# A hybrid decoder layer whose tile context schedules on the timeline machine model

## The chip, the cores and the metric

The kernel runs on one core of one Trainium2 chip. The metric is the device time of one execution in microseconds (us); lower is better. The time of the kernel before is the median of three runs.

## The reference

One layer of a decoder trunk: 1024 tokens, width 1024, float32. Both head groups read the same normalised input through one projection; after them come an output projection, a gated feed-forward network of width 2816 and a gated embedding, each added to the residual, and a last norm.

```python
hn = rms_norm(x, norm_mix_w[i])
proj = (hn @ w_in[i]).astype(jnp.float32)
...
y_ret = retention(q, k, v)            # 4 heads of 128, chunks of 128 tokens
y_ret = head_norm(y_ret) * ret_norm_w[i] * silu(ret_gate)
y_rw = rwkv7_mix(proj[..., RET_COLS:], ...)   # 8 heads of 64, a state per head over all tokens
mixed = jnp.concatenate([y_ret, y_rw], axis=-1)
x = x + mixed @ w_o[i]
hf = rms_norm(x, norm_ffn_w[i])
x = x + (silu(hf @ w_gate[i]) * (hf @ w_up[i])) @ w_down[i]
hp = rms_norm(x, norm_ple_w[i])
x = x + (p[i] @ w_ple_up[i]) * sigmoid(hp @ w_ple_gate[i])
return rms_norm(x, final_norm_w)
```

## The kernel before

Channels lie on the partitions, tokens along the free dimension, and the tokens are taken in two halves of 512. A float32 value of the dense products is split into a high and a low part (`split`, lines 246 to 248: ScalarE copies the high part at L247, VectorE or GpSimd subtracts it at L248), and a product is three matmuls: high times high, high times low, low times high. All matmuls are issued at L189 (`mm`), transposes at L193 (`tr`), all transfers on SyncE's queue.

There are two kinds of work in the first part of the program. The dense products (`dense`, tile names d<-x, d<-rr, d<-mix, d<-hT in the trace) need only weights and an operand in SBUF. The eight RWKV groups (`rwkv_group`: a pair of heads, half of the tokens) and the eight retention tasks (`retention`: a head, half of the tokens) are chains of small steps: a matmul, an operation of VectorE or ScalarE on its result, the next matmul. In a group these are, by the names of the PSUM tiles, ss, pb (two), then a row-by-row inverse on VectorE alone (L643 and L645, 31 steps of two operations), pk (two), bo, pq (five), psm (two), pw (two), pmq (two) and pkh (two), then eight steps of the state (pZ from the state Sn, copies of the state at L748 and L749 into STb, the transpose pS, the scaled copy Sn at L753), and at the end py and pyt. Retention goes through rtp (two), rsc, rU, rY and ryt. Each group and each retention task ends with a store into mixd (L783, L874), from which `mix_load` fetches the operands of the output projection (d<-mix).

The order of the program is written by `weave` (line 127). It counts matmul time in `pe` and, by constants such as `WAIT`, `INVW` and `MIDW`, decides after which dense matmuls the next step of a group or of a task is emitted. It runs while the program is traced and knows nothing of the scheduler. What comes out is one list of instructions over all engines.

From this list the tile context makes the queues of the engines when it closes. Its scheduler plays the program on a model of the machine: whenever an engine of the model can take an instruction, it gets, of those whose operands the model has finished and for which there is a buffer, the first in the order of the program (moved up by the few `tc.high_priority` blocks, mainly for the weight loads, and held by `tc.issue_after` in two places). So an instruction whose operand is not finished on the model is passed by later ones, and the order reached on the model is the order of the queue on the chip. Which buffer of a pool a tile gets is settled in the same way. Before the change the model is the default one.

After the RWKV part come the second halves of the feed-forward network with its down products (`down`, tile pd), and the embedding's gate (pg) with the last norm (`finish`).

Of the kernel before, what the change touches and what calls it, by code (L numbers as in the profile page):

```python
# [13 lines left out]
PSUM = bass.MemoryType.PSUM  # L14
DRAM = bass.MemoryType.DRAM
# [14 lines left out]
# columns of the packed constants  # L30
# [7 lines left out]
# columns of the packed parameter vectors  # L38
# [43 lines left out]
# a group may enter a stage once the group before it has reached another  # L82
# [44 lines left out]
def weave(groups, tasks, dg, count, pe, done):  # L127
    """Emit the groups' instructions as their operands become ready, then those of the first ready task, dense work in between.

    groups: (name, generator, dense items it needs), in order; tasks: name -> (generator, dense items, names that come before it)"""  # L130
    n = len(groups)
    ready, stage = [0.0] * n, [0] * n
    now, seen, mixed = 0.0, pe[0], 0.0
    tasks = dict(tasks)
    due = {k: 0.0 for k in tasks}
    last = STAGE["done"]
    while True:
        step = None
        for i, (name, g, need) in enumerate(groups):
            if stage[i] == last:  # L140
                continue
            if i and stage[i - 1] < STAGE[AFTER[STAGES[stage[i]]]]:
                break
            if count[0] >= need and ready[i] <= now and f"low{name[-1]}" in done:
                step = i
                break
        task = None
        for k, (g, need, before) in tasks.items():
            if max(due[k], mixed if k[:3] == "mix" else 0.0) <= now and count[0] >= need and all(x in done for x in before):
                task = k  # L150
                break
        if step is not None:
            st, wait = next(groups[step][1])
            stage[step] = STAGE[st]
            if stage[step] == last:
                done.add(groups[step][0])
            now += pe[0] - seen
            ready[step] = now + wait * (WAIT1 if groups[step][0][-1] == "1" else WAIT)
        elif task is not None:
            wait = next(tasks[task][0], None)  # L160
            now += pe[0] - seen
            if wait is None:
                mixed = now + MIXW if task[:3] == "mix" else mixed
                done.add(task)
                del tasks[task]
            else:
                due[task] = now + wait * (RWAIT1 if task[:3] == "ret" and task[-1] == "1" else RWAIT)
        elif min(stage) == last and not tasks:
            return
        else:  # L170
            if next(dg, True):
                now += 100.0
            now += pe[0] - seen
        seen = pe[0]
# [3 lines left out]
def tile_hybrid_layer(ctx: ExitStack, tc: tile.TileContext, I, out):  # L178
# [66 lines left out]
    # a float32 value as two float32r parts that add up to it exactly  # L245
# [9 lines left out]
    def dense(items, count, done, eng):  # L255
        """items: (weights [128, 512 n] in float32, variants); a variant (gate, columns, operands, use) gives use() the sum over
        its 128 columns of weights^T operand, once the names in gate are done. Yields after a few matmuls, whether it had to wait."""
# [41 lines left out]
    def rsqrt(y, x, tmp):  # L299
        """y = x ** -0.5 in place of x for positive x: a guess from the exponent, then Newton's steps"""  # L300
        V.tensor_scalar(out=tmp.bitcast(I32), in0=x.bitcast(I32), scalar1=1, scalar2=None, op0=ALU.logical_shift_right)
        V.tensor_scalar(out=y.bitcast(I32), in0=tmp.bitcast(I32), scalar1=-1.0, scalar2=1597463007.0, op0=ALU.mult, op1=ALU.add)
        V.tensor_scalar(out=x, in0=x, scalar1=-0.5, scalar2=None, op0=ALU.mult)
        for _ in range(3):
            V.tensor_tensor(out=tmp, in0=y, in1=y, op=ALU.mult)
            V.tensor_tensor(out=tmp, in0=tmp, in1=x, op=ALU.mult)
            V.scalar_tensor_tensor(out=y, in0=tmp, scalar=1.5, in1=y, op0=ALU.add, op1=ALU.mult)

    # RMS norm over the channels, which lie on the partitions
# [8 lines left out]
    def norm_rs(acc, parts, R):  # L318
        """R = 1 / sqrt(mean + eps) in all partitions; parts: room for the sums"""
        split(acc, *parts)  # L320
        norm_mm(*parts, R)
# [12 lines left out]
    def raw_split(raw, w, hi, lo):  # L334
        """the parts of raw times the norm's weight"""
        act(hi, raw, AF.Copy, scale=w)  # L336
        return V.scalar_tensor_tensor(out=lo, in0=raw, scalar=w, in1=hi.bitcast(F32), op0=ALU.mult, op1=ALU.subtract)

    def slabs(name):
        """[128, (kt, hi | lo, 512 tokens)]"""  # L340
        return slab.tile([P, KT, 2, HS], F32R, tag="s", name=name)
# [7 lines left out]
    # =================== input norm, input projection, RWKV and retention ===================  # L349
    with ExitStack() as s1:  # L350
# [22 lines left out]
        # x times the norm's weights; 1 / rms comes in when the projections leave PSUM  # L373
# [57 lines left out]
        def lerp(h, ps, i, t):  # L431
            """token shift with mu of tile i, token half h"""
            g = evac("pn")
            V.tensor_tensor(out=g, in0=ps, in1=Rx[h], op=ALU.mult)
            ps = g
            act(t, ps, AF.Copy, scale=pv(OMU + i))
            mu = pv(MU + i)
            if h == 0:
                edge[i] = sm.tile([P, 1], F32, tag="edge", name="edge", bufs=6)
                act(edge[i], ps[:, HS - 1:HS], AF.Copy, scale=mu)  # L440
            else:
                V.tensor_tensor(out=t[:, 0:1], in0=t[:, 0:1], in1=edge.pop(i), op=ALU.add)
            V.scalar_tensor_tensor(out=t[:, 1:HS], in0=ps[:, 0:HS - 1], scalar=mu, in1=t[:, 1:HS], op0=ALU.mult, op1=ALU.add)
# [24 lines left out]
        def low(h):  # L468
            """decay, in-context rate and gate of all heads from their low-rank parts"""
# [14 lines left out]
            # the high part beside the low one: one pass over 128 rows for both  # L484
# [34 lines left out]
        # block-diagonal holders; the zero blocks are written once  # L519
# [33 lines left out]
        def rwkv_group(p, hf):  # L553
            """a pair of heads over 8 chunks of 64 tokens; yields (stage, ns until the next matmuls can start)"""
# [11 lines left out]
            def headsum(ps, t):  # L566
                """sum of t over the channels of a head"""
# [11 lines left out]
            # decay and normaliser  # L579
# [35 lines left out]
            # products inside the chunks  # L615
# [25 lines left out]
            # inverse of the unit triangular blocks of 32 rows  # L641
# [32 lines left out]
            # two chunks at a time, then each head's rows to their place  # L674
# [20 lines left out]
            # merge to 64 rows  # L695
# [16 lines left out]
            # the chunk as an affine map: S' = P_C (M S + Kf V), y = Q S + Hy V  # L712
# [9 lines left out]
            for g in range(2):  # L722
# [8 lines left out]
                # M and Q take the room of their factor  # L731
# [6 lines left out]
            # the state (before P_C, transposed) and the output: [(h, v), (k | t)] of each chunk  # L738
# [18 lines left out]
            # head norm in token-major form, bonus, gate  # L757
# [34 lines left out]
        def retention(h, a):  # L792
            """a head over four chunks of 128 tokens; yields ns until the next matmuls can start"""
# [26 lines left out]
            # the scores take the room of v, the states that of k, the output that of the token-major k  # L820
# [13 lines left out]
            # the state before each chunk  # L834
# [25 lines left out]
            # (qs y - mean) / sqrt(var + eps) with the moments of y  # L860
# [16 lines left out]
        # =================== the dense products in an order that feeds the groups ===================  # L877
# [3 lines left out]
        # the embedding's operands, in the room of the retention  # L881
# [20 lines left out]
        def project(ct, use, halves):  # L902
            n = len(items)

            def var(h):
                def fin(ps):
                    # the first sums wait in PSUM for 1 / rms
# [31 lines left out]
        # the last heads' first token half before their second one: the operands of the output projection take its room  # L939
# [13 lines left out]
        def mix_load(h, k):  # L953
            """operands of the output projection, token half h"""
# [38 lines left out]
        def ffn0(f, then=None):  # L993
            """the first token half of the hidden layer, kept in DRAM"""
# [57 lines left out]
        def ffn1(f):  # L1052
# [13 lines left out]
            def up(ps):  # L1066
# [6 lines left out]
                if i == FC - 1:  # L1073
# [3 lines left out]
                    if c == NC - 2:  # L1077
                        # the first token half of the last part, so that its norm has time
# [13 lines left out]
        def fetch(c, step):  # L1092
            """a part of the last product's operands for part c: the first half's hidden layer and the weights"""
# [44 lines left out]
    # =================== the rest of the dense products ===================  # L1138
# [20 lines left out]
    def gate_weights(n):  # L1159
        """the weights of the embedding's gate"""  # L1160
# [44 lines left out]
    def gated(d, a, b, o, up):  # L1205
        """the embedding into the residual, its square and the product with the last norm's weights"""
# [17 lines left out]
    def settle():  # L1224
        """what is due one product later"""
# [8 lines left out]
    for a, b in passes:  # L1234
        h, n = a // HS, b - a
        t = slice(a - h * HS, b - h * HS)
        for d in range(KT):
# [19 lines left out]
            if b == S and d == KT - 1:  # L1257
                # Sqrt's table ahead of its use
# [65 lines left out]
```

## Time and profile before

| | |
|---|---|
| runs, us | 1630.67, 1626.79, 1630.40 |
| median, us | 1630.4 |
| span of the profiled execution, us | 1630.8 |
| TensorE busy, share of the span | 1519.8 us, 93% |
| VectorE busy | 1118.9 us, 69% |
| ScalarE busy | 689.5 us, 42% |
| GpSimd busy | 286.4 us, 18% |
| mean granted TensorE clock, share of full speed | 0.983 |
| instructions | 21374 |

The profiled execution is one of its own; its span is 0.4 us above the median, and no other time is given for it. In the profile PE is TensorE's matmul, PEld its weight load, DVE VectorE, ACT ScalarE, POOL GpSimd and SPq SyncE's queue. Matmuls are pipelined: the record of one is longer than its distance from the next, so busy time is a union of overlapping records. An idle time stands with the instruction that ended it, and with what released that instruction.

### The profile page before, as it was taken

Reading aid. Unit: us, or ns where it says so; the run is one execution under the profiler, and the core shown is the slowest. Engines: PE = TensorE matmul, PEld = TensorE weight load, DVE = VectorE, ACT = ScalarE, POOL = GpSimd, SP = SyncE. Lnnn points to the kernel's source line nnn. Section 1 sums busy time; section 2 is a strip of 40 time slices with the busy share of each in tenths; the row PEclk is TensorE's granted clock in tenths of the full one; section 3 lists DMA queues with packets and bytes.
Section 4 is the critical chain, followed back from the end, with each engine's and each line's share of the span. In section 5 each row is a group of like instructions: output and inputs, shape, how many; then the busy total and the mean of one; then the engine's idle time right before and its main releaser. Section 6 shows DMA issues by size and latency. Waiting matters only on the chain.

```text
span 1630.8 us, 21374 instructions
## 1 busy us (share of the span) xinstructions
PE 1519.8 (93%) x7406; PEld 1237.5 (76%) x7406; DVE 1118.9 (69%) x2364; ACT 689.5 (42%) x1383; POOL 286.4 (18%) x232
## 2 busy tenths in 40 slices
PE   7999999998888889889899999999999999999994
PEld 5777778786766668767677778788888888788894
DVE  7669796959798697894955545855555554556776
ACT  6655444443635547354253234522222222224554
POOL 7410111021222123323233320000000000000012
PEclk9999999999999999999999999999999999999997
DMA  6544242333534655243333545422222223321222
GB/s 204 168 160 154 91 130 82 111 119 101 194 118 130 211 162 176 69 150 101 117 124 111 167 144 171 155 93 85 84 85 82 73 79 97 104 78 46 72 84 78
DMA packets 108763, 194.06 MB, mean 119 GB/s; under 512 B 12272, under 2 KB 16496, under 8 KB 108656
## 3 DMA queue, kind: packets, MB, share of 16 engines
q1 hardware_dynamic: 108656, 192.71, 37.1%
q8 instruction: 58, 0.95, 0.2%
q14 instruction: 49, 0.40, 0.1%
HBM read 151.24 MB, written 41.42 MB: 118 GB/s over the span
## 4 chain that ended last, share of the span: by engine, by line
PE 54%; DVE 25%; DMA 8%; ACT 7%; issue 4%; POOL 2%; SPq 1%; DVEq 0%; ACTq 0%; POOLq 0%
PE d L189 30%; PE pd L189 14%; DVE tmp L643 4%; PE pg L189 3%; DVE R L645 3%; POOL lo L248 2%; DMA st<-in_w_in_dram 1%; DMA st<-in_w_up_dram 1%; ACT hi L247 1%; DVE lo L248 1%; DMA st<-mixd 1%; DVE Dm L637 1%; DMA st<-in_w_gate_dram 1%; PE pb L189 1%; PE pkh L189 1%
## 5 line engine op out<-in xcount | busy, mean ns | idle before, releaser
L189 PE MATMUL d<-hT,hi 128*128 128x512 f32 x1408 | 449.7, 399 | 6.5 <-ACT hi L247 4.0
L189 PE MATMUL d<-x,hi 128*128 128x512 f32 x960 | 322.7, 411 | 9.0 <-ACT x L336 6.7
L247 ACT ACTIVATE hi<-st 128x512 fp32r<-128x512 f32 x298 | 187.6, 629 | 314.0 <-PE d L189 142.7
L189 PEld LDWEIGHTS d<-hT,hi 128*128 128x128 f32 x1408 | 261.5, 190 | 57.8 <-ACT hi L247 6.6
L248 POOL TENSOR_TENSOR lo<-st,hi 128x512 fp32r<-128x512 f32 x139 | 194.1, 1397 | 597.6 <-ACT hi L247 529.6
L189 PE MATMUL d<-hT,lo 128*128 128x512 f32 x704 | 278.7, 396 | 2.8 <-POOL lo L248 2.2
L189 PE MATMUL pd<-h 128*128 128x512 f32 x1056 | 241.8, 389 | 0.0
L189 PEld LDWEIGHTS pd<-h 128*128 128x128 f32 x1056 | 198.2, 188 | 41.1
L189 PEld LDWEIGHTS d<-x,hi 128*128 128x128 f32 x960 | 179.1, 194 | 43.6 <-ACT x L336 6.7
L189 PE MATMUL d<-x,lo 128*128 128x512 f32 x480 | 194.0, 404 | 2.3 <-POOL lo L248 2.3
L248 DVE TENSOR_TENSOR lo<-st,hi 128x512 fp32r<-128x512 f32 x159 | 110.7, 697 | 109.4 <-ACT hi L247 108.9
L1116 DVE TENSOR_TENSOR x<-x,pd 128x512 f32<-128x512 f32 x176 | 120.5, 687 | 92.7 <-PE pd L189 91.8
L189 PEld LDWEIGHTS d<-hT,lo 128*128 128x128 f32 x704 | 133.6, 190 | 35.6 <-POOL lo L248 5.0
L247 ACT ACTIVATE h<-xr 128x512 fp32r<-128x512 f32 x66 | 38.4, 624 | 194.6 <-PE pd L189 176.7
L1198 POOL TENSOR_TENSOR x<-x,xr 128x256 f32<-128x256 f32 (+1 forms) x18 | 19.8, 1130 | 561.6 <-DVE xr L328 561.6
L189 PEld LDWEIGHTS d<-x,lo 128*128 128x128 f32 x480 | 93.1, 194 | 22.1 <-POOL lo L248 4.2
L643 DVE TENSOR_TENSOR tmp<-Dt,R 128x248 f32<-128x248 f32 (+30 forms) x248 | 89.8, 362 | 3.2
L645 DVE TENSOR_TENSOR R<-R,tmp 128x248 f32<-128x248 f32 (+30 forms) x248 | 82.7, 334 | 3.3
L189 PE MATMUL d<-mix,hi 128*128 128x512 f32 x256 | 82.1, 400 | 1.6 <-ACT hi L247 1.5
L189 PEld LDWEIGHTS d<-mix,hi 128*128 128x128 f32 x256 | 48.1, 192 | 11.7 <-ACT hi L247 1.9
L248 DVE TENSOR_TENSOR h<-xr,h 128x512 fp32r<-128x512 f32 x66 | 42.8, 689 | 14.0 <-ACT h L247 13.9
L1004 POOL TENSOR_TENSOR g<-g,R 128x512 f32<-128x512 f32 x22 | 29.2, 1325 | 125.6 <-DVE g L1003 122.8
(284 smaller groups left out, 2159.8 us busy)
## 6 DMA issues: line engine op xcount, KB each, us to landing
st<-in_w_gate_dram SPq DMA_DIRECT2D x88, 256.0 KB, 2.9
st<-in_w_up_dram SPq DMA_DIRECT2D x88, 256.0 KB, 2.8
st<-in_w_in_dram SPq DMA_DIRECT2D x86, 256.0 KB, 2.9
xr<-in_w_down_dram SPq DMA_DIRECT2D x44, 256.0 KB, 3.4
retd<-rt SPq DMA_DIRECT2D x32, 256.0 KB, 2.6
rr<-retd SPq DMA_DIRECT2D x32, 256.0 KB, 3.4
st<-in_w_o_dram SPq DMA_DIRECT2D x32, 256.0 KB, 3.0
rkvd<-rkvt SPq DMA_DIRECT2D x24, 256.0 KB, 2.2
```

The costliest lines, as they stand in the source:

```text
L189: return nc.tensor.matmul(ps, lhsT, rhs, start=start, stop=stop)
L247: act(hi, src, AF.Copy)
L248: (eng or V).tensor_tensor(out=lo, in0=src, in1=hi.bitcast(F32), op=ALU.subtract)
L637: V.tensor_tensor(out=Dm, in0=d0v[:, 0].rearrange("p u t -> p t u").unsqueeze(2).broadcast_to([P, 32, 4, NU]), in1=d0v[:, 1].rearrange("p ...
L643: V.tensor_tensor(out=tmp[:, :, 0:i], in0=Dt[:, i:i + 1, 0:i].broadcast_to([P, 8, i]), in1=R[:, :, i:i + 1].broadcast_to([P, 8, i]), op=AL ...
L645: V.tensor_tensor(out=R[:, :, 0:i], in0=R[:, :, 0:i], in1=tmp[:, :, 0:i], op=ALU.subtract)
L1004: G.tensor_tensor(out=g, in0=g, in1=R0[0], op=ALU.mult)
L1116: V.tensor_tensor(out=x1, in0=x1, in1=ps, op=ALU.add)
L1198: (V if b == S and d % 3 < 2 else G).tensor_tensor(out=x1[d][:, a:b], in0=x1[d][:, a:b], in1=R, op=ALU.mult)
```

## The change

One argument is added where the tile context is opened. The scheduler described above then plays the program on the timeline machine model instead of the default one. The traced list of instructions is the same, and so are all operands, tiles, pools, priorities and constants; the order of every engine's queue, the choice of buffers and the waits that follow from both are worked out anew. The rest of the diff takes away comments and docstrings.

```diff
-    with tile.TileContext(nc) as tc:
+    with tile.TileContext(nc, schedule_with_timeline_sim=True) as tc:
         tile_hybrid_layer(tc, aps, out)
```

## Rows read from the trace of the kernel before

**Rows 1.** Stretches: us, busy PE, PEld, DVE, ACT, POOL (instructions), granted clock, DMA.

```profile
0.00:120.00 120.00, 108.33 (x427) 81.88 (x428) 82.19 (x104) 76.75 (x131) 53.16 (x52) 0.99 0.55 179
120.00:326.00 206.00, 193.24 (x1012) 154.46 (x1010) 172.66 (x473) 94.52 (x226) 27.26 (x22) 0.99 0.35 113
326.00:571.00 245.00, 217.79 (x1165) 175.22 (x1165) 191.77 (x497) 119.07 (x278) 52.50 (x40) 0.98 0.45 146
571.00:815.00 244.00, 217.33 (x1109) 176.59 (x1108) 194.51 (x517) 111.61 (x242) 73.99 (x55) 0.97 0.41 129
815.00:978.00 163.00, 153.61 (x754) 123.69 (x755) 84.46 (x190) 61.96 (x129) 56.74 (x44) 0.99 0.44 136
...
1105.00:1480.00 375.00, 374.73 (x1645) 307.60 (x1644) 200.14 (x301) 92.80 (x158) 0.00 (x0) 1.00 0.26 82
...
1570.00:1631.00 61.00, 40.22 (x327) 39.46 (x326) 43.87 (x68) 28.33 (x55) 19.75 (x18) 0.84 0.21 74
```

**Rows 2.** Chain that ended last, one piece: start, us, what, count.

```profile
1101.85 21.76 PE pd L189 x96
```

**Rows 3.** TensorE's groups, 120 to 978 us: busy, mean ns | idle before, releasers.

```profile
L189 PE MATMUL d<-hT,hi 128*128 128x512 f32 x640 | 212.8, 410 | 4.0 <-ACT hi L247 4.0
...
L189 PE MATMUL rY<-rr 128*128 128x128 f32 x112 | 19.8, 294 | 7.9 <-DVE rmisc L856 6.3 <-DVE rmisc L846 1.6
L193 PE MATMUL pS<-cst,STb 128*128 128x128 f32 x60 | 19.3, 322 | 19.4 <-DVE STb L749 18.6
...
L189 PE MATMUL pmq<-BA,Wbd 128*128 128x128 f32 x128 | 17.3, 278 | 6.5 <-DVE BA L734 3.5 <-ACT Gbd L720 3.0
...
L193 PE MATMUL rtp<-cst,rr 128*128 128x128 f32 x64 | 10.9, 292 | 4.0 <-ACT rr L826 4.0
...
L189 PE MATMUL bo<-hs,onesr 128*128 128x512 f32 x16 | 7.4, 471 | 6.3 <-DVE hs L248 4.9 <-ACT hs L247 1.3
L193 PE MATMUL pyt<-cst,yn 128*128 128x128 f32 x32 | 5.5, 285 | 3.8 <-DVE yn L776 2.0 <-DVE R L645 1.8
...
L193 PE MATMUL ryt<-cst,rr 128*128 128x128 f32 x32 | 5.0, 278 | 4.7 <-ACT rr L868 4.7
```

**Rows 4.** One step of the state on the chain that ended last.

```profile
876.26 0.33 PE pS L193
876.59 1.39 PE d L189 x6
877.98 0.45 PE pZ L189 x4
878.42 0.70 PE d L189 x3
879.12 0.20 PE pS L193
```

**Rows 5.** Timeline of TensorE in another group's state: a transpose that waits.

```profile
561.48 0.33 PE L193 MATMUL pS<-cst,STb 128*128 128x128 f32 x1 [0.75 <-DVE STb L749]
```

**Rows 6.** Timeline: the last two loads of mixd, and the matmuls that need them.

```profile
923.49 0.32 SPq L252 DMA_DIRECT2D st<-mixd  x1
...
963.77 0.33 SPq L252 DMA_DIRECT2D st<-mixd  x1
...
965.32 0.61 PE L189 MATMUL d<-mix,hi 128*128 128x512 f32 x2
...
967.94 0.50 PE L189 MATMUL d<-mix,hi 128*128 128x512 f32 x1 [0.17 <-DVE mix L248]
```

**Rows 7.** SyncE's queue: who waited for whom, us in total, times, longest.

```profile
SPq L252 <- POOL lo L248: 267.2, 121, 8.8
```

**Rows 8.** Timeline of GpSimd and VectorE inside one inverse.

```profile
143.30 1.28 POOL L248 TENSOR_TENSOR lo<-st,hi 128x512 fp32r<-128x512 f32 x1 [2.14 <-ACT hi L247]
...
143.37 1.40 DVE L643 TENSOR_TENSOR tmp<-Dt,R 128x160 f32<-128x160 f32 x1
144.80 0.33 DVE L645 TENSOR_TENSOR R<-R,tmp 128x160 f32<-128x160 f32 x1
```

## The prediction, made before the change was timed

> **What bounds the kernel now.** I read the stretches first, because the program has stages with different limits [rows 1]. From 1105 to 1480 us TensorE is busy for 374.73 of 375 us at full granted clock: the dense products of the second half, in which the reader is to see that no order of the queues can give anything. The chain that ended last says the same in another way: one piece there holds 96 matmuls in 21.76 us, which is 0.2267 us for each matmul of 512 columns [rows 2]. From 120 to 978 us, where the RWKV groups and the retention run between the dense products, TensorE is busy for 193.24 + 217.79 + 217.33 + 153.61 = 782.0 of 858 us, and VectorE for 172.66 + 191.77 + 194.51 + 84.46 = 643.4. So TensorE stands idle for 76.0 us there while no engine is full. The first 120 us hold 11.7 us of such idle time and the last 61 us 20.8; both are a fixed start (loads, first norm) and a fixed end (last norm) with little beside them to reorder. The stage from 120 to 978 us is the one that the change reaches.
>
> The second view is TensorE's groups in that stage, with the idle time before each and what ended it [rows 3]. The reader is to see that the idle time stands before the small matmuls of the chains, not before the dense ones: pS 19.4, rY 7.9, pmq 6.5, bo 6.3, ryt 4.7, rtp 4.0 and pyt 3.8 us, together 52.6 of the 76.0, each ended by a result of VectorE or ScalarE. The largest dense group, d<-hT, waited 4.0 us in 640 matmuls. In all these places the next dense matmul stood behind the waiting one in TensorE's queue and did not pass it. So the idle time is a matter of order: the scheduler took the chain's operand for finished earlier than the chip finished it.
>
> **The change part by part.** The comments cost nothing: they make no instruction. The model of the machine adds and removes no operation, so the busy sums stay, and every gain or loss is a change of waits. What moves is the order of all five queues. I cost them in turn.
>
> TensorE's queue, gain. The state of a group shows both kinds of order in one trace. In one step there are three dense matmuls (0.70 us) ahead of the transpose pS and six (1.39 us) behind it, and pS starts without a wait: the step takes 879.12 - 876.26 = 2.86 us, nearly all of it matmuls [rows 4]. In another group pS stands too early and TensorE waits 0.75 us for the copy into STb, time for 0.75 / 0.2267 = 3.3 dense matmuls [rows 5]. If the new order puts as much dense work ahead of each pS as the first kind has, the 19.4 us of pS go. No row shows how the other model times an operation, so this is bounded from both sides: from nothing (the same order) to all 52.6 us of the seven groups, and for everything in the stage 76.0. I take 19.4, the row in which the trace itself holds the better order; the other six groups (33.2 us) have no such pattern, so I count nothing for them and keep them for the range.
>
> What is late next after such a gain: the dense matmuls come earlier, and so must their weights and the room in PSUM. A weight load on SyncE's queue waits for its buffer, 267.2 us in 121 waits, up to 8.8 us each [rows 7]. This is hidden now: the largest dense group has lost 4.0 us over its 640 matmuls [rows 3]. SyncE's stores and loads are reordered too; one store that comes to stand ahead of a weight load and waits as long as the longest of those waits would cost up to 8.8 us if the cover were gone. I count it at nothing, since 19.4 us spread over 858 is 2%, and keep half of 8.8 within the range.
>
> TensorE's queue, loss. The opposite move is a dense matmul put ahead of a chain matmul that was ready. It does not idle TensorE at that moment; it lengthens the chain by 0.2267 us, and costs time only when the chain is what the output projection waits for. The cover is in the last loads of mixd [rows 6]. The load at 963.77 us feeds a matmul at 967.94, with 0.17 us of wait, so load, split and matmul take 4.2 us; this is the last retention task, whose steps stand among dense matmuls in the order of the program and move along with them. The last RWKV group's load went out at 923.49 and would have been ready at 927.7, while its first reader is at 965.32: 37.6 us of slack. A slip of the groups below that costs nothing.
>
> VectorE's, ScalarE's and GpSimd's queues. VectorE is busy for 75% of the stage, so an evacuation or a split moved ahead of a step of the chain costs that step one operation, and the same slack covers it. One row shows a dearer case. While GpSimd subtracted a low part in 1.28 us, a step of the inverse took 1.40 us where the next one, of the same size, took 0.33 [rows 8]: 1.07 us lost on VectorE. [...]
>
> The sum, against the profiled execution's span of 1630.8 us: 1630.8 - 19.4 = 1611.4 us. The median of the runs is 0.4 us below that span, so I forecast 1611 us. Less than 0.3% (4.9 us) is about what a measurement of this kernel can tell from no change.
>
> **The rivals.** First, the chain falls behind dense work, and the kernel is slower. The eight groups have 21 places each at which TensorE takes up a result outside the state (ss 1, pb 2, pk 2, bo 1, pq 5, psm 2, pw 2, pmq 2, pkh 2, py and pyt 2), 168 in all, and pS and pZ with 60 each: 288. One dense matmul more at each is 288 x 0.2267 = 65.3 us; less the slack of 37.6 the output projection starts 27.7 us later, since the dense products ahead of it have run out: 1658 us. It decides from 37.6 / 288 = 0.13 us for each place on, about one matmul at every second. With three matmuls at each, the three of one split product, it is 195.9 - 37.6 = 158 us more, 1789. For it speaks that dense matmuls are nearly always ready, so any model that sees a chain's result a little late puts one ahead; against it that the idle time of [rows 3] says the present order errs the other way.
>
> Second, the order errs further in the present direction: the chain's matmuls come to stand earlier still, and the seven waits double. That is 52.6 us more, 1683 us. For it: nothing in the trace says on which side of the old model the new one lies.
>
> Third, more operations of the inverse meet GpSimd. There are 22 + 40 + 55 + 44 = 161 GpSimd instructions in the stage [rows 1]; if every one delayed a step of the chain by 1.07 us it would be 172.3 us, less 37.6 of slack 134.7, so 1765 us. It decides from 36 more such meetings on. Against it: GpSimd's share is 210 of 858 us, and most of it must have fallen beside other work.
>
> Fourth, the change hardly alters the order where it counts. The order of the program gives the rank in both cases, and a queue changes only where the models disagree on what is finished. Then it is 1630 us, within 0.3%.
>
> Fifth, the better order reaches all chain groups: 1630.8 - 52.6 = 1578 us.
>
> **How the numbers follow.** Forecast, about 1611 us (1591 to 1625): 0.42. All seven groups, 1578: 0.05. No change: 0.14. Chain behind dense, one matmul: 0.23; three matmuls: 0.07. Waits doubled: 0.06. GpSimd's collisions: 0.03. Faster by over 0.3% is 0.47, within 0.3% 0.14, slower 0.39. The forecast's own range ends below at three quarters of the seven groups, 1630.8 - 39.5 = 1591, and above at 1625, where the bound of no change begins. As both signs are likely, the whole range must reach the other side: it runs from 1590 to 1684, which takes in the first rival at one matmul and the second, and leaves out the fifth, the three matmuls and most of the third, some 0.15.
>
> **What would show it.** If the steps are right, TensorE's idle time from 120 to 978 us falls from 76.0 to about 57, with the pS group near nothing, more dense matmuls ahead of each pS, and the first d<-mix of the second half some 19 us before 965 us; the stage of 1105 to 1480 us keeps its 0.2267 us for each matmul, and all busy sums stay. The first rival shows as small waits before the chain's matmuls and one long wait at the output projection, with the last group's load of mixd close ahead of it. The second shows as the same groups with larger waits. The third shows as a larger busy time of L643 and L645. The prediction is wrong if the idle time of the seven groups stays or grows, or if it goes and the output projection does not start earlier.

## The result and the profile after

The kernel after takes 1747.35 us (median of four runs, 1745.41 to 1749.03) where the kernel before takes 1630.28 (median of four): a ratio of 1.0729, with a 95% interval of 1.0706 to 1.0751. It is slower by 117 us. I had forecast 1611 us and a range up to 1684. The profiled execution of after has a span of 1747.2 us, 116.4 above that of before.

The work is the same: 7406 matmuls in both, and VectorE, ScalarE and GpSimd are busy for 1127.8, 688.6 and 284.3 us, each within 9 us of before. TensorE's busy time, though, rises from 1519.8 to 1570.3 us and its idle time from 111.0 to 176.9: 50.5 + 65.9 = 116.4 us, the whole loss. The first view is the table of stretches, which answers [rows 1] (us, busy PE, PEld, DVE, ACT, POOL with instructions, granted clock, DMA share, GB/s).

```profile
0.00:120.00 120.00, 100.58 (x392) 76.43 (x393) 79.29 (x101) 72.60 (x123) 51.01 (x50) 0.96 0.50 165
120.00:326.00 206.00, 202.65 (x996) 167.31 (x995) 147.27 (x339) 79.55 (x177) 35.68 (x29) 0.98 0.40 132
326.00:571.00 245.00, 190.72 (x941) 158.23 (x940) 180.84 (x547) 95.84 (x237) 30.60 (x26) 0.80 0.28 90
571.00:815.00 244.00, 203.90 (x974) 167.04 (x974) 182.57 (x429) 112.67 (x247) 56.87 (x43) 0.85 0.41 134
815.00:978.00 163.00, 138.44 (x656) 114.21 (x657) 102.85 (x248) 68.46 (x156) 46.61 (x36) 0.87 0.34 108
978.00:1105.00 127.00, 110.91 (x524) 90.98 (x524) 47.51 (x124) 35.54 (x70) 37.15 (x29) 0.93 0.39 126
1230.00:1600.00 370.00, 370.00 (x1634) 306.35 (x1633) 200.04 (x301) 94.39 (x160) 0.00 (x0) 1.00 0.26 83
```

The reader is to see a feast and a famine. From 120 to 326 us TensorE is fuller than before (202.65 against 193.24 us), while VectorE does less (147.27 against 172.66): dense products run, and the chains don't get on. From 326 us on TensorE is idle for 54, 40 and 25 us in the next three stretches, where it was idle for 27, 27 and 9, and its granted clock falls to 0.80, 0.85 and 0.87, where it was 0.97 to 0.99. The dense tail is as full as before. The page's row of the granted clock in 40 slices shows where the dips are, first before, then after:

```profile
PEclk9999999999999999999999999999999999999997
PEclk9999999997668699796996998999999999999998
```

The feast in detail is one step of the state of the first group (timeline of all engines; lines left out are dense matmuls and work of other chains). It answers [rows 4].

```profile
215.16 0.39 PE L189 MATMUL pZ<-BA,Sn 128*128 128x128 f32 x2
...
216.07 0.23 DVE L749 COPY STb<-pZ 64x64 f32<-64x64 f32 x1
...
216.32 0.62 PE L189 MATMUL d<-x,hi 128*128 128x512 f32 x2
...
220.20 0.39 PE L189 MATMUL d<-x,lo 128*128 128x512 f32 x1
...
220.43 0.27 PE L193 MATMUL pS<-cst,STb 128*128 128x128 f32 x1
...
220.74 0.37 ACT L753 ACTIVATE Sn<-pS,PC 128x128 f32<-128x128 f32 x1 [3.09 <-PE pS L193]
...
225.34 0.39 PE L189 MATMUL pZ<-BA,Sn 128*128 128x128 f32 x2
```

The copy into STb is done at 216.30 us and pS starts at 220.43; nothing waits, TensorE simply has dense matmuls ahead of it. The next two rows count them (stretches, dense matmuls alone): 19 ahead of pS, of which one was running when the copy ended, and 20 ahead of the next pZ.

```profile
216.35:220.40 4.05, 4.05 (x19) 3.17 (x17) 2.27 (x1) 0.00 (x0) 1.00 0.38 124
220.70:225.30 4.60, 4.60 (x20) 3.64 (x20) 0.58 (x1) 0.00 (x0) 1.00 0.30 106
```

So a step takes 225.34 - 215.16 = 10.2 us. In the kernel before the same group has its first and its eighth pS at these times (timeline of TensorE):

```profile
190.59 0.33 PE L193 MATMUL pS<-cst,STb 128*128 128x128 f32 x1 [0.83 <-DVE STb L749]
...
212.55 0.33 PE L193 MATMUL pS<-cst,STb 128*128 128x128 f32 x1
```

That is 21.96 us for seven steps, 3.1 us each; the 2.86 us of [rows 4] are a step of the last group. The first group's store into mixd goes out at 301.3 us where it went at 233.5. The trace shows no overtaking here: pS's operand had been ready for 4.1 us, and pS passed none of the 19.

The famine follows. The first row below is the stretch from 395.8 to 503.2 us, the second the same stretch for dense matmuls alone:

```profile
395.80:503.20 107.40, 66.72 (x313) 54.74 (x311) 86.46 (x303) 47.00 (x122) 4.77 (x5) 0.67 0.24 79
395.80:503.20 107.40, 0.00 (x0) 0.00 (x0) 3.84 (x6) 0.00 (x0) 0.67 0.24 79
```

For 107 us TensorE has no dense matmul at all; only chains run, one result after the other, at a granted clock of 0.67. What ends it stands on SyncE's queue, at ScalarE and at TensorE (timelines; L252 loads a staging buffer, L783 is a group's store):

```profile
385.66 0.38 SPq L252 DMA_DIRECT2D st<-in_w_in_dram  x1
...
428.72 0.32 SPq L252 DMA_DIRECT2D st<-mixd  x1
...
494.84 0.38 SPq L783 DMA_DIRECT2D mixd<-Y  x1
...
498.73 0.32 SPq L252 DMA_DIRECT2D st<-mixd  x1
499.10 5.76 SPq L252 DMA_DIRECT2D st<-in_w_in_dram  x3
```

```profile
502.65 0.62 ACT L247 ACTIVATE hi<-st 128x512 fp32r<-128x512 f32 x1
```

```profile
503.32 1.22 PE L189 MATMUL d<-x,hi 128*128 128x512 f32 x2 [0.25 <-DVE L L586]
```

A load of mixd and a load of weights use the same two staging buffers (tile st). The weight loads stop at 385.66 us and go on at 499.10, right behind the load of mixd that had to wait for the third group's store. ScalarE has the high part of the first new weights ready at 503.27 us, and TensorE's first dense matmul starts at 503.32; the row names VectorE's L586, which ended at that moment and whose result this matmul doesn't read. There are six such stops of 26 to 113 us between 385 and 1053 us, all ended by a load of mixd; in the kernel before none in this stage is longer than 21 us. The stretches without a dense matmul (longer than 10 us, begun between 100 and 1050 us) add up to 268 us, in six pieces; before there is none.

In the famine the chains' matmuls wait for VectorE, and ryt for ScalarE, as the groups of TensorE show (120 to 1105 us), which answers [rows 3]:

```profile
L193 PE MATMUL pS<-cst,STb 128*128 128x128 f32 x60 | 19.9, 332 | 24.2 <-DVE STb L749 24.2
L189 PE MATMUL pmq<-BA,Wbd 128*128 128x128 f32 x128 | 18.1, 283 | 0.1
L193 PE MATMUL pyt<-cst,yn 128*128 128x128 f32 x32 | 8.2, 408 | 28.2 <-DVE yn L776 9.0 <-DVE rmisc L306 7.5 <-DVE tmp L643 7.0
L193 PE MATMUL ryt<-cst,rr 128*128 128x128 f32 x32 | 8.2, 392 | 9.9 <-ACT rr L868 9.9
```

### The profile page after: what moved, and what is told of

Its sections match the earlier page's. It is cut to its first block, busy times and chain, and to the rows that moved or that the text cites. A ratio compares the mean times of both kernels' runs of the same rounds, so it can differ in the third digit from the quotient of the medians.

```text
span 1747.2 us, 21375 instructions
## 1 busy us (share of the span) xinstructions
PE 1570.3 (90%) x7406; PEld 1297.7 (74%) x7406; DVE 1127.8 (65%) x2364; ACT 688.6 (39%) x1383; POOL 284.3 (16%) x232
## 4 chain that ended last, share of the span: by engine, by line
PE 47%; DVE 8%; ACT 2%; issue 1%; DMA 0%; POOL 0%; DVEq 0%; SPq 0%; ACTq 0%
PE d L189 27%; PE pd L189 14%; PE pg L189 3%; DVE tmp L643 1%; DVE R L645 1%; DVE x L1209 0%; DVE o L1207 0%; PE pw L189 0%; PE pkh L189 0%; PE pmq L189 0%; DVE acc L1217 0%; PE pk L189 0%; PE pZ L189 0%; DVE Dm L637 0%; ACT XR L682 0%
## 5 line engine op out<-in xcount | busy, mean ns | idle before, releaser
L189 PE MATMUL d<-x,hi 128*128 128x512 f32 x960 | 316.4, 409 | 13.6 <-ACT x L336 8.4
L189 PEld LDWEIGHTS d<-hT,hi 128*128 128x128 f32 x1408 | 267.1, 191 | 68.7 <-ACT hi L247 12.5
L248 POOL TENSOR_TENSOR lo<-st,hi 128x512 fp32r<-128x512 f32 x139 | 187.6, 1352 | 549.3 <-ACT hi L247 484.1
L189 PE MATMUL pd<-h 128*128 128x512 f32 x1056 | 245.7, 389 | 0.0
L189 PEld LDWEIGHTS d<-x,hi 128*128 128x128 f32 x960 | 183.6, 195 | 56.3 <-ACT x L336 8.4
L645 DVE TENSOR_TENSOR R<-R,tmp 128x248 f32<-128x248 f32 (+30 forms) x248 | 87.7, 354 | 5.9
L643 DVE TENSOR_TENSOR tmp<-Dt,R 128x248 f32<-128x248 f32 (+30 forms) x248 | 86.7, 350 | 5.4
L189 PE MATMUL d<-mix,lo 128*128 128x512 f32 x128 | 50.3, 393 | 1.5 <-DVE lo L248 1.4
```

What stands on the lines that cost most here:

```text
L189: return nc.tensor.matmul(ps, lhsT, rhs, start=start, stop=stop)
L248: (eng or V).tensor_tensor(out=lo, in0=src, in1=hi.bitcast(F32), op=ALU.subtract)
L643: V.tensor_tensor(out=tmp[:, :, 0:i], in0=Dt[:, i:i + 1, 0:i].broadcast_to([P, 8, i]), in1=R[:, :, i:i + 1].broadcast_to([P, 8, i]), op=AL ...
L645: V.tensor_tensor(out=R[:, :, 0:i], in0=R[:, :, 0:i], in1=tmp[:, :, 0:i], op=ALU.subtract)
```

## The experiments

**What the theories count.** For every matmul I counted, in TensorE's queue, the matmuls that come later in the program but stand ahead of it. The kernel before has 15,292 such overtaken places in all, the kernel after 152,725; for pS it is 9 on average before and 190 after. The theory: the timeline model takes many ready dense matmuls before it sees a chain's result, and TensorE's order alone makes the loss. The rivals: the order of VectorE and ScalarE makes it; or the model's durations.

**The window of the model.** The timeline model has a window for each engine: the number of instructions that it takes ahead of the one it executes. It is a setting of the scheduler's software, and no run here shows such a number on the chip. The kernel after leaves it as it comes, at 35 for TensorE and 12 for the others; a kernel can overwrite it before it opens the tile context, here with 16, 8, 4, 2 and 1. Nothing else is changed.

```diff
     lay = _lay(inputs)
+    from concourse import hw_specs
+    hw_specs.TRN2Spec.ENG_ISSUE_QUEUE_DEPTH[mybir.EngineType.PE] = 4
     nc = bacc.Bacc("TRN2", target_bir_lowering=False, num_devices=1)
```

Expected of 16:

> Theory 1 (TensorE's window): 16 instead of 35 leaves 93,234 overtaken places, so 1630 + 117 x 77,942 / 137,433 = 1696 us, between 1670 and 1720; less if the first part of the slip is covered by the 37.6 us of slack that the kernel before has. Theories 2 (other engines) and 3 (durations in the model): about 1747 us.

Expected of 8:

> TensorE's window 8 instead of 35: 40,440 overtaken places (window 4: 23,521 and 1626.5 us; window 16: 93,234 and 1699.5 us). Without a threshold, on the line from the kernel before to the kernel after: 1630 + 117 x 25,148 / 137,433 = 1651 us, between 1643 and 1665. With a slack that covers a first part of the slip of the chains (the 37.6 us of the prediction): the time stays at that of window 4, 1620 to 1635 us.

Expected of 4:

> Theory 1 (TensorE's window): the timeline model lets TensorE take 35 instructions ahead of the one it executes, so ready dense matmuls are committed ahead of a chain matmul that becomes ready a little later. With 4 instead of 35 the matmuls overtaken in TensorE's queue fall from 152,725 places in all to 23,521 (the kernel before has 15,292). By the line from 15,292 (1630 us) to 152,725 (1747 us) this gives 1630 + 117 x 8,229 / 137,433 = 1637 us; between 1620 and 1645. Theory 2 (the order of VectorE, ScalarE and GpSimd is at fault): their windows are left at 12, so most of the loss stays, above 1700 us. Theory 3 (the durations that the model gives to operations are at fault): nothing changes, 1747 us.

Expected of 2:

> TensorE's window 2 instead of 35: 16,990 overtaken places, next to the 15,292 of the kernel before. Theory 1 (places overtaken): 1631 us by the line, and not over 1640. If a smaller window only puts the chain's matmuls too early, so that TensorE waits for their operands (the rival of doubled waits): slower than with a window of 4 (1626.5 us), by 10 us or more.

Expected of 1:

> TensorE's window 1: 4,826 overtaken places, fewer than the kernel before, so nearly the order of the program. Theory 1 in its plain form (fewer places overtaken are always better): 1621 us. The rival of waits (a chain's matmul that stands ahead of the dense ones makes TensorE wait for VectorE and ScalarE, as in the pS row of the kernel before): the idle time before the chain's matmuls at least doubles, 52 us more, 1683 us or above. I expect the second: there is a best place between too early and too late.

| TensorE's window in the model | overtaken places | dense matmuls ahead of the first group's py | stretches without dense matmuls, us | time, us | ratio to before, interval |
|---|---|---|---|---|---|
| default model (before) | 15,292 | 633 | 0 | 1630.3 | 1 |
| 35 (after) | 152,725 | 893 | 268 | 1747.35 | 1.0729 (1.0706 to 1.0751) |
| 16 | 93,234 | 774 | 149 | 1699.51 | 1.0423 (1.0394 to 1.0453) |
| 8 | 40,440 | 692 | 52 | 1647.82 | 1.0114 (1.0081 to 1.0147) |
| 4 | 23,521 | 649 | 11 | 1626.52 | 0.9973 (0.9952 to 0.9994) |
| 2 | 16,990 | 638 | 0 | 1624.63 | 0.9960 (0.9938 to 0.9982) |
| 1 | 4,826 | 633 | not counted | 2021.25 | 1.2383 (1.2363 to 1.2404) |

One number of the model moves the time from 1625 to 1747 us, in the order of the overtaken places, and within 11 us of the line that I had drawn through before and after (1696, 1651, 1637 and 1631 expected). With 35, 16 and 8, each 100 us without dense matmuls come with a loss of 44, 46 and 37 us against the kernel before of the same comparison. The model's durations, the other thing that the change exchanges, do not make the loss by themselves: with them and a window of 2 the kernel is 0.4% faster than before. One small part does not follow the window. In the first 120 us TensorE is busy for 100.58 us where it was busy for 108.33 [rows 1], and with a window of 2 it is 101.55:

```profile
0.00:120.00 120.00, 101.55 (x395) 75.94 (x396) 79.46 (x99) 72.09 (x123) 49.80 (x50) 0.97 0.51 163
```

No run tells where this comes from; over the whole program a window of 2 makes up for it. A window of 8 also speaks against a slack that is used up first; its reading stands in the next section.

A window of 1 shows the other end. The chain's matmuls stand ahead of the dense ones, and TensorE waits for their operands (groups of TensorE, 120 to 1300 us):

```profile
L193 PE MATMUL pS<-cst,STb 128*128 128x128 f32 x60 | 23.4, 390 | 117.6 <-DVE STb L749 116.6
```

Here pS waits for 117.6 us where [rows 3] have 19.4. I had expected about 1683 us or above; it is 2021. The best order lies between the two, and it is narrow.

**The windows of the other engines.** TensorE keeps 35; the rest gets 2.

```diff
+    for e in (mybir.EngineType.Activation, mybir.EngineType.DVE, mybir.EngineType.Pool, mybir.EngineType.SP):
+        hw_specs.TRN2Spec.ENG_ISSUE_QUEUE_DEPTH[e] = 2
```

> TensorE's window stays at 35, those of ScalarE, VectorE, GpSimd and SyncE's queue go from 12 to 2. Theory 1 (TensorE's window): 148,557 overtaken places on TensorE, so 1743 us, between 1730 and 1760. Theory 2 (evacuations and steps of the inverse in the wrong order on VectorE and ScalarE): most of the loss goes, below 1680 us. Theory 3: 1747 us.

Measured: 1749.07 us, ratio 1.0727 (1.0695 to 1.0759), the same as after. With TensorE's window at 35, the other engines' windows play no part.

**TensorE's order by itself.** Each of TensorE's instructions is held behind the one that precedes it in the other kernel's queue (an edge that fixes the order of issue and waits for nothing). The model in use then orders the other queues around that. First the default model with TensorE's order of after:

```diff
         tile_hybrid_layer(tc, aps, out)
+        _pin(nc, tc, mybir.EngineType.PE, ORDER_PE)
...
+    for a, c in zip(mine, mine[1:]):
+        tc.add_manual_dep(c, a.name, info, reason="pinned order")
```

> The kernel before with its default model, and only TensorE's queue held to the order that it has after the change; the default model orders the other queues around it. Theory 1 (TensorE's order alone makes the loss): 1735 to 1760 us. Theory 2 (the other engines' order makes it): near 1630 us, at most 1660. Both in part: in between.

Then the timeline model with TensorE's order of before:

> The kernel after with its timeline model, and only TensorE's queue held to the order of the kernel before; the timeline model orders the other queues around it. Theory 1 (TensorE's order alone makes the loss): 1620 to 1645 us. Theory 2 (the other queues' order under the timeline model costs time by itself): above 1680 us.

| | other queues by the default model | other queues by the timeline model |
|---|---|---|
| TensorE's order of before | 1630.3 (before) | 1676.13, ratio 1.0272 (1.0239 to 1.0305) |
| TensorE's order of after | 1794.18, ratio 1.1008 (1.0969 to 1.1046) | 1747.35 (after) |

Both times are over 30 us above what I had expected (1735 to 1760 and 1620 to 1645), and the table says why. TensorE's order costs 163.9 us in one column and 71.2 in the other, 117.5 on average, about the loss. The order of the other queues costs 45.8 us in the first row and gains 46.8 in the second, nothing on average. It matters by whether it is the one that goes with TensorE's order. The average is a way of counting: the two columns differ by 92.7 us, so TensorE's order is the larger cause here, but not alone. The famine does follow it: the stretches without a dense matmul add up to 272 us with the order of after under the default model, and there is none with the order of before under the timeline model. The price of a mismatch shows in the waits of TensorE, first for the timeline's queues around the old order, then for the default model's queues around the new order (groups, 120 to 1105 us):

```profile
L193 PE MATMUL pS<-cst,STb 128*128 128x128 f32 x60 | 18.8, 314 | 26.5 <-DVE STb L749 26.3
L189 PE MATMUL bo<-hs,onesr 128*128 128x512 f32 x16 | 7.8, 498 | 12.2 <-DVE hs L248 9.8 <-ACT hs L247 2.4
L193 PE MATMUL ryt<-cst,rr 128*128 128x128 f32 x32 | 5.9, 316 | 14.5 <-ACT rr L868 14.5
```

```profile
L193 PE MATMUL pS<-cst,STb 128*128 128x128 f32 x60 | 20.5, 342 | 30.2 <-DVE STb L749 30.0
L193 PE MATMUL ryt<-cst,rr 128*128 128x128 f32 x32 | 8.2, 394 | 28.3 <-ACT rr L868 28.3
```

The first is to be read against [rows 3], where pS, bo and ryt wait for 19.4, 6.3 and 4.7 us; the second against the kernel after, where pS and ryt wait for 24.2 and 9.9.

**VectorE's and ScalarE's order by itself.** The same edges, for these two queues and not for TensorE, under the timeline model.

```diff
         tile_hybrid_layer(tc, aps, out)
+        _pin(nc, tc, mybir.EngineType.DVE, ORDER_DVE)
+        _pin(nc, tc, mybir.EngineType.Activation, ORDER_ACT)
```

> The kernel after with its timeline model, VectorE's and ScalarE's queues held to the order of the kernel before, TensorE's queue left to the model: 64,141 overtaken places on TensorE, since its matmuls follow the order of the results that they take up. Theory 1 (TensorE's order sets the time, through the places overtaken): 1630 + 117 x 48,849 / 137,433 = 1672 us, between 1650 and 1700. Theory 2 (VectorE's and ScalarE's order sets it): near 1630, at most 1645 us.

Measured: 1742.41 us, ratio 1.0677 (1.0656 to 1.0697). It doesn't go back, which is against theory 2, but it isn't the 1672 us that I had worked out from the overtaken places either. The waits have moved to the dense matmuls. All their groups together wait for 63.8 us from 120 to 1105 us (15.4 in before, 15.8 in after), and this is the largest:

```profile
L189 PE MATMUL d<-x,hi 128*128 128x512 f32 x714 | 241.9, 423 | 30.5 <-ACT hi L247 14.8 <-DVE rt L452 10.4 <-DVE pn L434 3.1
```

The stretches without them add up to only 42 us, in four pieces, so this loss of 112 us is not the famine of the kernel after. The count of places therefore serves for comparing windows of the same model and no further: between two queues that were not made together it misses the waits.

**The gate.** Do the staging buffers cause the famine, or is it only seen there? A load of mixd now lands in the low half of its own mix tile, and is split in place:

```diff
-            load_split(mixd[k, :, half(h)], mixs[h][:, k, 0, :], mixs[h][:, k, 1, :])
+            lo = mixs[h][:, k, 1, :]
+            load_split(mixd[k, :, half(h)], mixs[h][:, k, 0, :], lo, st=lo.bitcast(F32))
```

On the kernel after:

> The kernel after, but a load of mixd lands in the low half of its own mix tile and no longer in one of the two staging buffers that the weight loads use. In the kernel after the weight loads stop six times for 26 to 113 us and go on right behind a load of mixd, and in these stretches no dense matmul runs. Theory A (this gate is the cause: with weight loads that pass the mixd loads TensorE has dense work beside the chains and the time goes back): 1640 to 1690 us. Theory B (the gate is only the place where late chains become visible; the cause is that the chains stand behind dense matmuls): the dense matmuls go still further ahead (271,474 overtaken places instead of 152,725), the chains come later, and TensorE runs dry once at the output projection instead: 1740 us or above.

On the kernel before, as the control:

> The control for the run above: the kernel before with the same change of the mixd loads. Its weight loads never stop for more than 21 us in this stage, so both theories expect 1630 us within 0.5%.

On the timeline model with a window of 2:

> The timeline model with TensorE's window 2 (1624.6 us) and the mixd loads in their own tile. Nothing but the weight loads that stand behind a load of mixd can gain; these gaps are under 23 us and dense matmuls run through most of them: 1615 to 1630 us. If dense work that is free to run ahead always harms the chains: above 1635 us.

The kernel after with this edit takes 1704.02 us, ratio 1.0460 (1.0424 to 1.0496): between the two expectations, so both theories hold in part. About 117 - 75 = 42 us of the loss go with the shared staging buffers, or 35 if the 7 us that the control gains are taken off. This is a net figure, since TensorE's order changes too: the overtaken places rise from 152,725 to 271,474, and yet the kernel is faster. The other 75 stay, and the table of stretches shows where:

```profile
571.00:815.00 244.00, 199.54 (x941) 163.63 (x941) 198.30 (x474) 104.63 (x234) 63.33 (x48) 0.82 0.33 105
815.00:978.00 163.00, 154.35 (x797) 128.92 (x796) 121.83 (x298) 65.66 (x141) 62.02 (x47) 0.99 0.41 129
978.00:1105.00 127.00, 100.74 (x462) 80.44 (x461) 61.46 (x145) 49.09 (x106) 8.38 (x6) 0.87 0.39 125
```

The famine has not gone but moved. It is 192 us in four stretches now, and two of them (555.7 to 604.7 and 1017.0 to 1058.7 us) lie between matmuls of the output projection, which needs the chains' results themselves. The chains are as late as in after: the last group's store goes out at 1052.8 us (1049.8 in after, 921.4 before).

The control is 1621.54 us, ratio 0.9949 (0.9931 to 0.9967); I had expected no change, and the edit gives 0.5% by itself. With a window of 2 it is 1612.27 us, ratio 0.9889 (0.9860 to 0.9918). This is the fastest version here, 1.1% below before and 7.7% below after.

## Why the prediction was wrong

**The stage was right.** From 1230 to 1600 us TensorE is busy for 370.00 of 370 us, and all of the loss arises before. The busy sums of VectorE, ScalarE and GpSimd stayed, as I had said; TensorE's did not.

**The step that failed is the gain at pS.** I took 19.4 us off for it. I let the idle time of [rows 3] say that the default model sees the chain's results too early, and gave the new model the pattern of [rows 4] as the likeliest. That pattern was the old model's own. Nothing in the trace of before tells on which side the new model errs, and it errs on the other: 19 and 20 dense matmuls ahead of a chain's matmul, where [rows 4] have three and six. The row that should have gone to nothing rose from 19.4 to 24.2 us, and the seven groups together from 52.6 to 79.6 us, which the prediction had named as a sign of being wrong. The case of three quarters of the seven groups did not come either: pmq fell from 6.5 to 0.1 us, bo and rY by 3.4 and 1.0, but pyt rose from 3.8 to 28.2.

**The first rival was the mechanism, but its sizes and what was to show it were off.** It named the cause (dense matmuls ahead of a ready chain matmul). It was to show as one long wait at the output projection; what came is six stretches without dense matmuls, the longest of 107 us, from 395.7 us on. Its price per place was one or three dense matmuls; measured are 19 to 20 in the first group, and 893 - 633 = 260 more dense matmuls by the end of that group. Later groups can't be pushed back as far, since the dense work that may run ahead is used up: between the py of the second and of the third group there is not one dense matmul in the queue. I read this as what bounds the loss, in place of places times price (288 places at 19 would be 288 x 19 x 0.2267 = 1241 us); no run tests it by itself. That 117 us lies between my 28 for one matmul and 158 for three is chance.

**The slack of 37.6 us was not there.** I read it from the last two loads of mixd [rows 6], as the distance of the last group from the output projection. But each group's load of mixd stands ahead of weight loads that use the same staging buffers, in the kernel before too (SyncE's queue, right behind that very load):

```profile
923.92 4.93 SPq L252 DMA_DIRECT2D st<-in_w_gate_dram  x2
```

So every group has a reader of its own, and its slack is that of the next dense product. A window of 8 fits this. The last group's store goes out at 938.4 us where it was 921.4, a slip of 17 us, less than half of that slack, and yet the kernel takes 19 us more. Weights had come late before that (SyncE's queue and TensorE, timelines, window of 8; L874 is a retention task's store):

```profile
489.21 0.54 SPq L874 DMA_DIRECT2D mixd<-rr  x1
492.39 0.38 SPq L252 DMA_DIRECT2D st<-mixd  x1
492.86 6.35 SPq L252 DMA_DIRECT2D st<-in_w_in_dram  x3
```

```profile
484.25 0.40 PE L189 MATMUL d<-x,lo 128*128 128x512 f32 x1
498.66 1.20 PE L189 MATMUL d<-x,hi 128*128 128x512 f32 x2
```

A store, a load of mixd, and only then the weights: 14 us without a dense matmul. The retention tasks moved too; their last store is at 974.2 us, 959.4 before.

**SyncE's queue was mis-sized.** I allowed half of one wait of 8.8 us for a weight load behind another transfer [rows 7]. One such stop lasted 113 us. The rule was stated in the prediction (a store or load that comes to stand ahead of a weight load); what I had not looked at is that its length is that of a late chain and not that of a transfer. The run with the mixd loads in their own tile puts some 42 us net on this term.

**The clock was left out.** 50.5 of the 116.4 us are busy time of TensorE, for the same 7406 matmuls. My sums used 0.2267 us for each matmul everywhere and had no term for a TensorE that runs at a lower granted clock (0.925 on average, 0.983 before); the last section has the rows.

**The start was not fixed.** I had set the first 120 us aside as a part with little to reorder. Its idle time rose from 11.7 to 19.4 us.

**The other rivals.** Waits did grow, as in the second rival, but as a consequence of the famine: with a window of 2 pS waits for 15.7 us, less than before. The third rival did not happen: the inverse (L643 and L645) is busy for 174.4 us, 172.5 before.

**What stays open.** How the 65.9 us of idle time and the 50.5 us of busy time hang together was not separated by a run: where the granted clock is low the chains' own matmuls are longer too (a matmul of pyt takes 421 ns in the stretch of 0.67 and 272 in the first group, medians), and a matmul that overlaps with no other adds its whole record to the busy time, where one of pd among others adds 0.2267 us [rows 2] of a record of 389 ns. Why the default model gains 0.5% from the mixd loads in their own tile I only argue: its weight loads, too, stood behind loads of mixd, for up to 21 us. And why a window of 35 puts 19 to 20 dense matmuls ahead of a chain's matmul, and not another number, was not shown.

## What to carry to other kernels

An order that a scheduler works out on a model is only as good as what the model thinks is finished, and the side on which it errs can be read in the new queues before any run: count, ahead of each step of a chain, the independent matmuls that come later in the program. The count ranks orders of one model between which nothing else differs, and only on the side of too late: the fewest places (a window of 1) gave the slowest kernel here. When independent work fills the gaps of a chain, running it early is no gain, because it is missing later; keep its lead small, here 638 matmuls at the first group's end instead of 893. Slack is read at the nearest reader of each intermediate result, shared buffers included, and not at the end of the chain.

## What the hardware showed that I had not expected

TensorE's granted clock fell where the loss arose. Its mean went from 0.983 to 0.925. From 395.8 to 503.2 us it was 0.67 while TensorE was busy for 66.72 of 107.4 us with small matmuls. From 120 to 326 us, with dense matmuls around the chains', it was 0.98. A matmul of pyt takes 408 ns on average in after and 285 before [rows 3]. Of the 32 in after, 28 stand in the six stretches without dense matmuls; the eight in the stretch of 0.67 take 421 ns (median), the four of the first group, at 296 us, take 272. So the matmuls of a chain that was left alone on TensorE took longer than those of a chain beside dense work. How much of the 117 us this makes was not shown.
